# A two-layer decoder trunk with four mixers: every engine's queue ordered by a simulated timeline, and the first block rearranged

## The chip, the cores and the metric

The kernel runs on one core of one Trainium2 chip. The metric is the device time of one execution in microseconds (us), from the program's start to its end on the core. Several engines work side by side, each through its own queue in order: PE (TensorE, matmuls and transposes), DVE (VectorE), ACT (ScalarE), POOL (GpSimd) and SP (SyncE, which here only issues DMAs). PEld is PE's loading of weights.

## The reference

The reference is a decoder trunk of two layers over 512 positions with 1,024 features, all in float32. In each layer:

```python
u = rmsnorm(h, norm_w[l])
proj = einsum('bsd,de->bse', u, w_in[l])
ret_p, diff_p, ssd_p, ml_p = split_cols(proj, ...)
ret_out = retention_mixer(...) * silu(rz)
diff_out = diff_attention_mixer(...) * silu(dz)
ssd_out = _rms(ssd_mixer(...) * silu(sz)) * ssd_norm_w[l]
ml_out = mlstm_mixer(...) * silu(mz)
mix = concatenate([ret_out, diff_out, ssd_out, ml_out])
h = h + einsum('bse,ed->bsd', mix, w_out[l])
```

After the second layer comes one more RMSNorm. All four mixers are causal; the kernel computes them in four chunks of 128 positions.

## The kernel before

**Tiles.** The four token tiles h0 to h3 (128 positions x 1,024 features) stay on the chip. The input projection of a layer is cut into blocks of 512 columns, and each block into eight weight tiles of 128 x 512. Float32 is made up from two parts: ACT casts a weight tile to a shorter format (`whi`, L357, or L360 with a scale for the output projection), and DVE subtracts that from the original to get the rest (`wlo`, L358 and L361). The same is done to the normalised activations (`uh` L347, `ul` L348), and to the mixers' results (`mh`, `ml`, L623). A product of two tiles is three matmuls, whi with uh, whi with ul, and wlo with uh, all recorded at L127; transposes are at L131. Raw weights come in by DMA from SP, two tiles each (L366, tile `raw`).

**What sets the order.** PE's order is written by hand. `drive` runs generators against a planner's clock that `mm` and `tr` advance, and `later` and `spawn` put pieces of a mixer at a planned time between the projections' matmuls. In the body of the kernel only PE is scheduled by hand (`manual_schedule`); DVE, ACT, POOL and SP get their order from the tile scheduler, which ranks instructions by priority, raised in places with `high_priority`. That order is fixed when the program is built: on the chip each engine takes its queue from the front and waits on semaphores.

**The first block.** `start` makes the first projection block, "mv", with its own order on all engines, since nothing is there to hide its loads. Its weight tiles come as `z` (0 to 7). For each token tile t, `squares(t)` is ACT's sum of squares (L390), `scale(t)` the statistics on DVE (L395, L397) with a power on POOL (L240), `mul(t)` the scaling on DVE (L404, two halves `e`), `trans(t)` the transposes on PE (L131) with the split into uh and ul. `hi(k)` and `lo(k)` make the two parts of weight tile k (L414, L418) on the engine that is named, and `run(pr[t], n)` issues the next n-1 steps of token t's matmuls. The strings in `orders` say in which order a token uses the high (h) and low (l) parts. `warm(n)` in `setup` issues n matmuls of ones (L127), whose result isn't used. Tables for later come after the weights: `rows` and `w` (used at L313 and L304) and the convolution's `cv` (L295, L298).

**Places in the body that the prediction speaks of.** In differential attention, `diff_av` transposes the attention weights on PE and copies them out of a bank of PSUM, on DVE for even t (L1157). A later projection matmul needs that bank. Near it on DVE are L361, the end of `diff_fin` (L1184, L1186), and the gating by silu (ACT L542, DVE L544). In the SSD mixer, each chunk has eight L950 on DVE (one for each head), an exponential on ACT (L952), and a product with the scores on DVE (L954, two halves), on which the matmuls into `psacc` wait. POOL works for the same mixer with L941, L967 and L980, and for the rotary embedding with L605, beside DVE's L604 and L606 and ACT's L602; DVE adds up the chunk's result at L978, L992 and L995. In the mLSTM mixer the same part is played by L839, L841 on ACT and L846. The last token's final norm is at L1296 to L1304.

Of the kernel before, what the change touches and what calls it, by code (L numbers as in the profile page):

```python
# [99 lines left out]
class Trunk:  # L100
# [21 lines left out]
    def mm(self, out, lhsT, rhs, start=True, stop=True, share=1.0, **kw):  # L122
        n = 1
        for d in rhs.shape[1:]:
            n *= d
        self.clk += max(n, 64 if lhsT.dtype == F32 else 256) / 2400.0 * (4 if lhsT.dtype == F32 else 1) * share
        self.nc.tensor.matmul(out, lhsT=lhsT, rhs=rhs, start=start, stop=stop, **kw)  # L127
# [71 lines left out]
    def setup(self):  # L199
        nc = self.nc  # L200
        self.h = [self.hp.tile([P, D], F32, name=f"h{t}") for t in range(NT)]
        row = self.t("raw", [1, D], bufs=2)
        nc.scalar.dma_start(out=row, in_=self.nrm[0:1, :])
        for half in range(2):
            hs = slice(half * 512, (half + 1) * 512)
            nc.sync.dma_start(out=self.h[0][:, hs], in_=self.x[0:P, hs])
        cst = self.cp.tile([P, C_W], F32, name="cst")
        nc.sync.dma_start(out=cst[:, 0:P], in_=self.cst[:, 0:P])
        self.rest = lambda: nc.sync.dma_start(out=cst[:, P:], in_=self.cst[:, P:])
        self.c = lambda o, w, p=P: cst[:p, o:o + w]  # L210
        self.ident = self.c(C_ID, P)
        self.ones = self.cp.tile([P, P], F32, name="ones")
        nc.vector.memset(self.ones, 1.0)
        self.nhalf = self.cp.tile([P, 8], F32, name="nhalf")
        nc.vector.memset(self.nhalf, -0.5)
        self.zrow = self.cp.tile([4, P], F32, name="zrow")
        nc.vector.memset(self.zrow, 0.0)


        p = self.psum()  # L220

        def warm(n):
            for _ in range(n):
                self.mm(p[:, 0:P], lhsT=self.ones, rhs=self.ones)
        warm(4)
        self.nw = [self.psum() for _ in range(2)]
        for half in range(2):
            self.mm(self.nw[half], lhsT=self.ones[0:1, :], rhs=row[:, half * 512:(half + 1) * 512])
        warm(3)
        self.free(p)  # L230

    def setup2(self):
# [140 lines left out]
    def start(self, evac):  # L373

        nc = self.nc
        E = mybir.EngineType
        b = BIDX["mv"]
        w = [[None, None] for _ in range(KD)]
        us, ms, rs = {}, {}, {}

        def run(g, n=None):
            for i, _ in enumerate(g):
                if n and i == n - 1:
                    return

        def squares(t):
            ms[t] = self.sm([P, 2])
            for half in range(2):
                junk = self.t("e", [P, 512], BF16, bufs=4)
                nc.scalar.activation(junk, self.h[t][:, half * 512:(half + 1) * 512], AF.Square,  # L390
                                     accum_out=ms[t][:, half:half + 1])

        def scale(t):
            m = self.sm([P, 1])
            nc.vector.tensor_scalar(m, ms[t][:, 0:1], EPS * D, None, ALU.add)  # L395
            m2 = self.sm([P, 1])
            nc.vector.tensor_scalar(m2, ms[t][:, 1:2], m, 1.0 / D, ALU.add, ALU.mult)  # L397
            rs[t] = self.sm([P, 1])
            self.rsqrt(rs[t], m2, 1)

        def mul(t):
            us[t] = [self.ev(), self.ev()]
            for half in range(2):
                nc.vector.scalar_tensor_tensor(us[t][half], self.h[t][:, half * 512:(half + 1) * 512], rs[t],  # L404
                                               self.nw[half], ALU.mult, ALU.mult)

        def trans(t):
            for half in range(2):
                self.norm_tr(t, half, us[t][half])
            self.done.add(("u", 0, t))  # L410

        def hi(k, eng=nc.scalar.copy):
            w[k][0] = self.t("whi", [P, 512], F32R, bufs=10)
            eng(out=w[k][0], in_=raw[k])  # L414

        def lo(k, eng=nc.vector):
            w[k][1] = self.t("wlo", [P, 512], F32R, bufs=10)
            eng.tensor_tensor(out=w[k][1], in0=raw[k], in1=w[k][0].bitcast(F32), op=ALU.subtract)  # L418

        with self.tc.manual_schedule(engines={E.Activation, E.DVE, E.Pool, E.SP}):  # L420
            self.setup()
            load = lambda t: nc.sync.dma_start(out=self.h[t], in_=self.x[t * P:(t + 1) * P, :])
            raw = []
            for k in range(KD):
                raw.append(self.t("z", [P, 512], bufs=8))
                nc.sync.dma_start(out=raw[k], in_=self.win[0, b, :, k, :])
                if k == 1:
                    load(1)
            load(2)
            load(3)  # L430
            self.rest()
            self.loads(0)

            orders = ["h0 h1 l0 l1 h2 h3 h4 h6 l2 h5 l4 l3 h7 l6 l5 l7", "h0 h1 h2 h3 l0 l1 l2 l3 h4 h5 h6 h7 l4 l5 l6 l7"]
            pr = [self.proj_tok("mv", evac, w, (t,), [(int(x[1]), ("hl".index(x[0]),)) for x in orders[min(t, 1)].split()])
                  for t in range(NT)]
            squares(0)
            scale(0)
            mul(0)
            hi(0, nc.vector.tensor_copy)  # L440
            trans(0)
            lo(0)
            hi(1)
            hi(2)
            hi(3)
            lo(1)
            run(pr[0], 6)
            squares(1)
            hi(4, nc.vector.tensor_copy)
            hi(6, nc.vector.tensor_copy)  # L450
            lo(4, nc.gpsimd)
            scale(1)
            lo(2)
            hi(5)
            hi(7)
            mul(1)
            lo(6, nc.gpsimd)
            lo(3)
            run(pr[0], 6)
            trans(1)  # L460
            lo(5)
            lo(7, nc.gpsimd)
            run(pr[0], 2)
            squares(2)
            run(pr[1], 4)
            run(pr[0])
            scale(2)
            mul(2)
            run(pr[1], 4)
            squares(3)  # L470
            trans(2)
            scale(3)
            mul(3)
            self.free(*self.nw, lag=3.0)
            run(pr[1])
            self.gates_w()
            run(pr[2], 8)
            trans(3)
            run(pr[2])
            run(pr[3])  # L480
            self.setup2()
        yield
# [873 lines left out]
```

## Time and profile before

| | us |
|---|---|
| three runs | 1043.56, 1045.69, 1046.55 |
| median | 1045.69 |
| the profiled execution's own time | 1043.91 |
| its span, first to last instruction | 1042.1 |
| mean granted clock of TensorE | 0.994 |

The profile shows one execution. An interval in brackets behind a row of its timeline is the time that the engine stood idle ahead of it, with what ended the wait: "[2.13 <-DVE w L1157]" is 2.13 us, ended by DVE's tile w at L1157. "x3" merges three like instructions in a row, and the duration then spans all of them. Names of engines with a q (POOLq) are the engine's sequencer.

### The profile page before, as it was taken

The numbers are of one execution on the slowest core, as the hardware profiler recorded it, in microseconds if no ns is written. First come the engines' busy times: TensorE is split into PE (matmuls) and PEld (weight loads), VectorE is DVE, ScalarE is ACT, GpSimd is POOL, SyncE is SP. The second block draws the span as 40 slices with busy tenths as digits, with TensorE's granted clock in tenths as the row PEclk, the third lists the DMA queues.
The fourth block names the chain that finished last, engine by engine and source line by source line (L and its number), as shares of the span: only waits on it lengthen the run. The fifth ranks groups of instructions, "written<-read, shape, count | busy, mean of one in ns | idle before, by whom it ended". The sixth has DMA issues, their size and how long they took to land.

```text
span 1042.1 us, 14190 instructions
## 1 busy us (share of the span) xinstructions
PE 1023.0 (98%) x5110; PEld 835.1 (80%) x5110; DVE 693.2 (67%) x1495; ACT 479.7 (46%) x1057; POOL 164.9 (16%) x204
## 2 busy tenths in 40 slices
PE   8999999999999999999999999999999999999997
PEld 6788888877778887878887888887777888878786
DVE  5588675567787867446655967666667786863454
ACT  4444336545455444433343542575444553553332
POOL 2000132101111233022000012210001112510301
PEclk9999999999999999999999999999999999999999
DMA  7324322322212413313122422233121233233112
GB/s 254 107 72 122 102 71 82 101 82 81 79 44 85 128 51 102 102 61 126 41 84 80 138 85 81 82 101 103 60 86 56 81 100 103 81 102 101 42 60 81
DMA packets 39144, 93.84 MB, mean 90 GB/s; under 512 B 3849, under 2 KB 16777, under 8 KB 38946
## 3 DMA queue, kind: packets, MB, share of 16 engines
q1 hardware_dynamic: 38064, 91.49, 28.7%
q10 hardware_dynamic: 1010, 1.45, 0.4%
q8 instruction: 40, 0.66, 0.3%
q14 instruction: 30, 0.25, 0.1%
HBM read 90.78 MB, written 2.15 MB: 89 GB/s over the span
## 4 chain that ended last, share of the span: by engine, by line
PE 90%; DVE 5%; issue 1%; ACT 1%; DMA 1%; POOL 0%; POOLq 0%; DVEq 0%; ACTq 0%
PE pspj L127 74%; PE psS L127 6%; PE psacc L127 6%; PE psS L131 4%; DMA raw<-in_w_in_dram 1%; DVE wlo L361 1%; DVE w L950 1%; DVE ft L606 0%; DVE z L1291 0%; DVE wlo L358 0%; DVE h L657 0%; DVE z L544 0%; ACT e L253 0%; DMA raw<-in_w_out_dram 0%; DVE wlo L418 0%
## 5 line engine op out<-in xcount | busy, mean ns | idle before, releaser
L358 DVE TENSOR_TENSOR wlo<-raw,whi 128x512 fp32r<-128x512 f32 x248 | 174.0, 721 | 67.4 <-ACT whi L357 61.8
L127 PE MATMUL pspj<-whi,uh 128*128 128x512 f32 x512 | 209.7, 410 | 0.0
L127 PE MATMUL pspj<-whi,ul 128*128 128x512 f32 x512 | 200.9, 392 | 0.0
L127 PE MATMUL pspj<-wlo,uh 128*128 128x512 f32 x512 | 197.7, 393 | 2.4 <-DVE wlo L418 2.2
L357 ACT CAST whi<-raw 128x512 fp32r<-128x512 f32 x248 | 147.8, 618 | 108.5 <-PE pspj L127 60.8
L127 PE MATMUL pspj<-uh,whi 128*128 128x512 f32 x448 | 179.2, 400 | 0.0
L127 PE MATMUL pspj<-uh,wlo 128*128 128x512 f32 x448 | 174.7, 390 | 0.0
L127 PE MATMUL pspj<-ul,whi 128*128 128x512 f32 x448 | 174.6, 390 | 0.0
L127 PEld LDWEIGHTS pspj<-wlo,uh 128*128 128x128 f32 x512 | 96.5, 189 | 25.1 <-DVE wlo L418 3.9
L127 PEld LDWEIGHTS pspj<-whi,uh 128*128 128x128 f32 x512 | 97.0, 189 | 22.4 <-issue 3.0
L127 PEld LDWEIGHTS pspj<-whi,ul 128*128 128x128 f32 x512 | 96.9, 189 | 17.8 <-DVE ul L348 0.4
L127 PE MATMUL pspj<-whi,mh 128*128 128x512 f32 (+1 forms) x260 | 105.2, 405 | 4.3 <-DVE w L1157 4.3
L240 POOL TENSOR_TENSOR s<-s,nhalf 128x4 f32<-128x4 f32 (+1 forms) x44 | 35.8, 813 | 417.5 <-DVE s L1181 122.9
L127 PE MATMUL pspj<-whi,ml 128*128 128x512 f32 (+1 forms) x260 | 101.4, 390 | 0.3
L127 PE MATMUL pspj<-wlo,mh 128*128 128x512 f32 (+1 forms) x260 | 101.2, 389 | 0.0
L127 PEld LDWEIGHTS pspj<-uh,wlo 128*128 128x128 f32 x448 | 84.1, 188 | 18.2
L127 PEld LDWEIGHTS pspj<-uh,whi 128*128 128x128 f32 x448 | 84.2, 188 | 17.4 <-issue 0.7
L127 PEld LDWEIGHTS pspj<-ul,whi 128*128 128x128 f32 x448 | 84.3, 188 | 16.0
L584 DVE SCALAR_TENSOR_TENSOR e<-pspj,cvh,e 128x511 f32<-128x511 f32 (+2 forms) x90 | 67.0, 744 | 9.6 <-ACT e L582 8.4
L602 ACT ACTIVATE e<-pspj 32x512 f32<-32x512 f32 x96 | 56.6, 589 | 20.0 <-PE pspj L127 18.7
L657 DVE TENSOR_TENSOR h<-pspj,h 128x512 f32<-128x512 f32 (+1 forms) x65 | 43.6, 678 | 28.7 <-PE pspj L127 28.3
L127 PEld LDWEIGHTS pspj<-whi,mh 128*128 128x128 f32 x260 | 49.3, 190 | 15.4 <-DVE w L1157 5.2
(221 smaller groups left out, 1406.4 us busy)
## 6 DMA issues: line engine op xcount, KB each, us to landing
raw<-in_w_in_dram SPq DMA_DIRECT2D x116, 512.0 KB, 3.9
raw<-in_w_out_dram SPq DMA_DIRECT2D x32, 512.0 KB, 3.5
bcm<-adr SPq DMA_DIRECT2D x16, 256.0 KB, 3.3
z<-in_w_in_dram SPq DMA_DIRECT2D x8, 256.0 KB, 6.6
bcm<-gdr SPq DMA_DIRECT2D x8, 256.0 KB, 3.8
out_dram<-z SPq DMA_DIRECT2D x7, 256.0 KB, 2.0
h<-in_x_dram SPq DMA_DIRECT2D x3, 512.0 KB, 6.5
cst<-in_consts_dram SPq DMA_DIRECT2D x1, 1035.0 KB
```

Of the source, the lines that this page charges most:

```text
L127: self.nc.tensor.matmul(out, lhsT=lhsT, rhs=rhs, start=start, stop=stop, **kw)
L131: self.nc.tensor.transpose(out, src, self.ident if ident is None else ident)
L240: self.nc.gpsimd.tensor_tensor(out=out, in0=m, in1=self.nhalf[:, :n], op=ALU.pow)
L357: nc.scalar.copy(out=hi, in_=raw)
L358: nc.vector.tensor_tensor(out=lo, in0=raw, in1=hi.bitcast(F32), op=ALU.subtract)
L361: nc.vector.scalar_tensor_tensor(lo, raw, scale, hi.bitcast(F32), ALU.mult, ALU.subtract)
L584: nc.vector.scalar_tensor_tensor(acc[:, s:], p[:, 0:S - s], w[:, 3 - s:4 - s], acc[:, s:], ALU.mult, ALU.add)
L602: nc.scalar.activation(x[q * 32:q * 32 + 32, :], p[o * 32:o * 32 + 32, :], AF.Copy, scale=scale)
L657: nc.vector.tensor_tensor(out=hs, in0=p, in1=hs, op=ALU.add)
L950: nc.vector.scalar_tensor_tensor(e[:, j * P:(j + 1) * P], ab[g][:, j, :], self.ncs[:, t, h:h + 1], self.cap, ALU.add, ALU.min)
```

## The change

The diff has three parts. First, `schedule_with_timeline_sim=True`: the tile scheduler now picks, on each engine that isn't ordered by hand, the next instruction by a simulated timeline of all engines instead of by priority alone. Second, `warm(3)` in `setup` goes, so three of the seven matmuls of ones. Third, the first block's hand-written order changes: token 0 takes h7 ahead of its low parts 4, 6 and 3, the other tokens take all high parts before all low ones, the low parts 4 and 6 on POOL are issued behind `mul(1)` and `trans(1)`, and low part 7 goes from POOL to DVE.

```diff
--- before.py
+++ after.py
@@ -226,7 +226,6 @@
         self.nw = [self.psum() for _ in range(2)]
         for half in range(2):
             self.mm(self.nw[half], lhsT=self.ones[0:1, :], rhs=row[:, half * 512:(half + 1) * 512])
-        warm(3)
         self.free(p)
 
     def setup2(self):
@@ -431,7 +430,7 @@
             self.rest()
             self.loads(0)
 
-            orders = ["h0 h1 l0 l1 h2 h3 h4 h6 l2 h5 l4 l3 h7 l6 l5 l7", "h0 h1 h2 h3 l0 l1 l2 l3 h4 h5 h6 h7 l4 l5 l6 l7"]
+            orders = ["h0 h1 l0 l1 h2 h3 h4 h6 l2 h5 h7 l4 l6 l3 l5 l7", "h0 h1 h2 h3 h4 h5 h6 h7 l0 l1 l2 l3 l4 l5 l6 l7"]
             pr = [self.proj_tok("mv", evac, w, (t,), [(int(x[1]), ("hl".index(x[0]),)) for x in orders[min(t, 1)].split()])
                   for t in range(NT)]
             squares(0)
@@ -448,19 +447,20 @@
             squares(1)
             hi(4, nc.vector.tensor_copy)
             hi(6, nc.vector.tensor_copy)
-            lo(4, nc.gpsimd)
             scale(1)
             lo(2)
             hi(5)
             hi(7)
             mul(1)
+            run(pr[0], 5)
+            trans(1)
+            lo(4, nc.gpsimd)
             lo(6, nc.gpsimd)
             lo(3)
-            run(pr[0], 6)
-            trans(1)
+            run(pr[1], 4)
             lo(5)
-            lo(7, nc.gpsimd)
-            run(pr[0], 2)
+            lo(7)
+            run(pr[0], 3)
             squares(2)
             run(pr[1], 4)
             run(pr[0])
@@ -1349,7 +1349,7 @@
     for i, (shape, dtype) in enumerate(_OUTS):
         args.append(nc.dram_tensor(f"out_{i}_dram", shape, mybir.dt.from_np(np.dtype(dtype)),
                                    kind="ExternalOutput").ap())
-    with tile.TileContext(nc) as tc:
+    with tile.TileContext(nc, schedule_with_timeline_sim=True) as tc:
         trunk_kernel(tc, args)
     r = _run(nc, [arrays], core_ids=[0])
     return r.results[0]["out_0_dram"]
```

PE's instructions are the same but for those three matmuls, and behind the first block they stand in the same order. The line numbers of the changed kernel are one lower from L230 to the rearranged lines of `start` (L418 is L417 there) and the same behind those. The numbers of tiles in its rows are lower by 3 outside the first block.

The first place is PE in the first block, from the warm-up on; `e` are the normalised halves, `psS` the transposes' banks, `pspj_174` (171 in the changed kernel) is token 0's sum and `pspj_251` (236) token 1's. Before, from the low parts of token 0 to its end and the transposes of token 1:

```order
L127 MATMUL pspj_174<-wlo_202,uh_75 128x512
L127 MATMUL pspj_174<-whi_204,uh_75 128x512
L127 MATMUL pspj_174<-whi_204,ul_76 128x512
L127 MATMUL pspj_174<-wlo_194,uh_75 128x512
L127 MATMUL pspj_174<-wlo_214,uh_75 128x512
L131 MATMUL psS_225<-cst,e_208 128x128 x4
L131 MATMUL psS_232<-cst,e_209 128x128 x4
L127 MATMUL pspj_174<-whi_206,uh_75 128x512
L127 MATMUL pspj_174<-whi_206,ul_76 128x512
L127 MATMUL pspj_174<-wlo_212,uh_75 128x512
L127 MATMUL pspj_251<-whi_148,uh_75 128x512
L127 MATMUL pspj_251<-whi_148,ul_76 128x512
```

And after:

```order
L127 MATMUL pspj_171<-wlo_197,uh_75 128x512
L127 MATMUL pspj_171<-whi_199,uh_75 128x512
L127 MATMUL pspj_171<-whi_199,ul_76 128x512
L127 MATMUL pspj_171<-whi_201,uh_75 128x512
L127 MATMUL pspj_171<-whi_201,ul_76 128x512
L131 MATMUL psS_216<-cst,e_203 128x128 x4
L131 MATMUL psS_223<-cst,e_204 128x128 x4
L127 MATMUL pspj_236<-whi_145,uh_75 128x512
L127 MATMUL pspj_236<-whi_145,ul_76 128x512
L127 MATMUL pspj_236<-whi_163,uh_75 128x512
L127 MATMUL pspj_236<-whi_163,ul_76 128x512
L127 MATMUL pspj_236<-whi_165,uh_75 128x512
```

In between token 0's high parts and the transposes of token 1 stood wlo_202, wlo_194 and wlo_214, the low parts 2, 4 and 3; now only wlo_197, the low part 2, stands ahead of them.

On DVE the end of the first block's stage for token 2 (`s` are its statistics, `cvh` and `cv` the convolution's table, `e_271` and `e_276` its normalised halves) read before:

```order
L418 TENSOR_TENSOR wlo_239<-z_118,whi_204 128x512
L395 TENSOR_SCALAR s_60_265<-s_55_246 128x1
L314 TENSOR_SCALAR aneg_457<-aneg_457 128x8
L397 TENSOR_SCALAR s_61_267<-s_55_246,s_60_265 128x1
L304 TENSOR_TENSOR w_448<-w_129 128x128
L404 SCALAR_TENSOR_TENSOR e_271<-h_81,s_62_269,psS_100 128x512
L404 SCALAR_TENSOR_TENSOR e_272<-h_81,s_62_269,psS_101 128x512
L295 TENSOR_SCALAR cvh_445<-cv_131 128x80
L298 TENSOR_SCALAR cv_131<-cv_131 128x1
```

And after:

```order
L417 TENSOR_TENSOR wlo_234<-z_111,whi_167 128x512
L417 TENSOR_TENSOR wlo_245<-z_115,whi_199 128x512
L417 TENSOR_TENSOR wlo_247<-z_119,whi_201 128x512
L394 TENSOR_SCALAR s_60_270<-s_56_252 128x1
L313 TENSOR_SCALAR aneg_454<-aneg_454 128x8
L303 TENSOR_TENSOR w_445<-w_126 128x128
L294 TENSOR_SCALAR cvh_442<-cv_128 128x80
L297 TENSOR_SCALAR cv_128<-cv_128 128x1
L396 TENSOR_SCALAR s_61_272<-s_56_252,s_60_270 128x1
L403 SCALAR_TENSOR_TENSOR e_276<-h_81,s_62_274,psS_100 128x512
L403 SCALAR_TENSOR_TENSOR e_277<-h_81,s_62_274,psS_101 128x512
```

The two rows of the convolution's table (L295, now L294, and L298, now L297) moved ahead of the second row of statistics and of L404 (now L403), and two more low parts are made by DVE ahead of them.

In ACT's row of the same stage the two casts of the next block's first raw weights (L357) moved ahead of the copy of token 0's result (L567) and of token 3's squares (L390); token 2's casts to uh (L347) stand behind all of these, as before.

The next place is DVE in the first layer's differential attention, around the copy at L1157 that PE waits for (`w_2424`, in the changed kernel `w_2421`). Before:

```order
L361 SCALAR_TENSOR_TENSOR wlo_2485<-raw_2478,cv_131,whi_2484 128x512
L361 SCALAR_TENSOR_TENSOR wlo_2491<-raw_2488,cv_131,whi_2490 128x512
L361 SCALAR_TENSOR_TENSOR wlo_2495<-raw_2488,cv_131,whi_2494 128x512
L1184 TENSOR_TENSOR s_696_2378<-s_696_2378,s_694_2372 128x4
L544 SCALAR_TENSOR_TENSOR z_2431<-e_2429,pspj_2264 128x512
L1186 TENSOR_TENSOR w_2381<-psacc_2014,s_696_2378 128x512
L544 SCALAR_TENSOR_TENSOR z_2456<-e_2454,pspj_2385 128x512
L1157 COPY w_2424<-psS_2422 128x128
L1138 RECIPROCAL s_708_2415<-rsum_2275 128x1
L1139 SCALAR_TENSOR_TENSOR s_659_2276<-s_708_2415,rsum_2275,nlam_454 128x1
L1141 SCALAR_TENSOR_TENSOR w_2399<-w_2400,s_659_2276,w_2399 128x512
L358 TENSOR_TENSOR wlo_2778<-raw_2775,whi_2777 128x512
```

And after:

```order
L1133 TENSOR_REDUCE s_703_2395<-psS_2399 128x1
L544 SCALAR_TENSOR_TENSOR z_2428<-e_2426,pspj_2261 128x512
L1184 TENSOR_TENSOR s_696_2375<-s_696_2375,s_694_2369 128x4
L360 SCALAR_TENSOR_TENSOR wlo_2482<-raw_2475,cv_128,whi_2481 128x512
L360 SCALAR_TENSOR_TENSOR wlo_2488<-raw_2485,cv_128,whi_2487 128x512
L1186 TENSOR_TENSOR w_2378<-psacc_2011,s_696_2375 128x512
L1157 COPY w_2421<-psS_2419 128x128
L360 SCALAR_TENSOR_TENSOR wlo_2492<-raw_2485,cv_128,whi_2491 128x512
L1138 RECIPROCAL s_708_2412<-rsum_2272 128x1
L544 SCALAR_TENSOR_TENSOR z_2453<-e_2451,pspj_2382 128x512
L1139 SCALAR_TENSOR_TENSOR s_659_2273<-s_708_2412,rsum_2272,nlam_451 128x1
L1141 SCALAR_TENSOR_TENSOR w_2396<-w_2397,s_659_2273,w_2396 128x512
```

Ahead of the copy stood four L361 since L1181, and now three; the second L544 (z_2456, now z_2453) stood ahead of it, and is now two rows behind.

The last place is the SSD mixer's last chunk in the first layer. DVE before, from L978 to the second half of L954 and what follows:

```order
L978 TENSOR_TENSOR w_3812<-psacc_3809,g_144_575 128x512
L992 TENSOR_TENSOR state_3818<-psS_3815,state_3818 128x512
L950 SCALAR_TENSOR_TENSOR w_3838<-bcm_3822,g_148_583,cap 128x128 x2
L995 TENSOR_TENSOR w_3731<-psacc_3800,w_3731 128x512
L950 SCALAR_TENSOR_TENSOR w_3838<-bcm_3822,g_148_583,cap 128x128 x2
L950 SCALAR_TENSOR_TENSOR w_3845<-bcm_3824,g_148_583,cap 128x128 x4
L358 TENSOR_TENSOR wlo_4095<-raw_4092,whi_4094 128x512
L604 SCALAR_TENSOR_TENSOR ft_3865<-pspj_3763,cst 128x512
L954 TENSOR_TENSOR w_3838<-w_3838,psS_3835 128x512
L954 TENSOR_TENSOR w_3845<-w_3845,psS_3835 128x512
L606 TENSOR_TENSOR ft_3865<-ft_3865,e_3860 128x512
L358 TENSOR_TENSOR wlo_4099<-raw_4092,whi_4098 128x512
```

And after:

```order
L978 TENSOR_TENSOR w_3809<-psacc_3806,g_144_572 128x512
L992 TENSOR_TENSOR state_3815<-psS_3812,state_3815 128x512
L950 SCALAR_TENSOR_TENSOR w_3835<-bcm_3819,g_148_580,cap 128x128 x4
L950 SCALAR_TENSOR_TENSOR w_3842<-bcm_3821,g_148_580,cap 128x128 x4
L995 TENSOR_TENSOR w_3728<-psacc_3797,w_3728 128x512
L357 TENSOR_TENSOR wlo_4092<-raw_4089,whi_4091 128x512
L357 TENSOR_TENSOR wlo_4096<-raw_4089,whi_4095 128x512
L604 SCALAR_TENSOR_TENSOR ft_3862<-pspj_3760,cst 128x512
L954 TENSOR_TENSOR w_3835<-w_3835,psS_3832 128x512
L954 TENSOR_TENSOR w_3842<-w_3842,psS_3832 128x512
L313 TENSOR_SCALAR aneg_5003<-aneg_5003 128x8
```

The split wlo_4099 (now wlo_4096) moved from behind both L954 to ahead of L604, and L995 from among the L950 to behind them. POOL at the same place, before:

```order
L605 TENSOR_TENSOR e_3782<-e_3782,cst 128x512
L941 TENSOR_TENSOR w_3833<-w_3831,g_133_516 128x512
L980 TENSOR_TENSOR w_3731<-w_3731,w_3812 128x512
L967 TENSOR_TENSOR w_3852<-w_3831,rows_127 128x512
L605 TENSOR_TENSOR e_3860<-e_3860,cst 128x512
L240 TENSOR_TENSOR s_1290_3957<-s_1289_3955,nhalf 128x1
```

And after:

```order
L605 TENSOR_TENSOR e_3779<-e_3779,cst 128x512
L980 TENSOR_TENSOR w_3728<-w_3728,w_3809 128x512
L941 TENSOR_TENSOR w_3830<-w_3828,g_133_513 128x512
L967 TENSOR_TENSOR w_3849<-w_3828,rows_124 128x512
L605 TENSOR_TENSOR e_3857<-e_3857,cst 128x512
L239 TENSOR_TENSOR s_1290_3954<-s_1289_3952,nhalf 128x1
```

L941 and L980 changed places. In the second layer the same rows move in the same way.

## The prediction

> **What bounds the kernel now.** I read the page first (busy time by engine, then the chain that ended last), then the waits of PE, then the windows table for the granted clock, and then the timeline where PE stood still.
>
> ```profile
> PE 1023.0 (98%) x5110; PEld 835.1 (80%) x5110; DVE 693.2 (67%) x1495; ACT 479.7 (46%) x1057; POOL 164.9 (16%) x204
> ...
> PE 90%; DVE 5%; issue 1%; ACT 1%; DMA 1%; POOL 0%; POOLq 0%; DVEq 0%; ACTq 0%
> ...
> PE pspj L127 <- DVE w L1157: 4.3, 2, 2.2
> PE psacc L127 <- DVE w L954: 3.1, 2, 1.6
> PE pspj L127 <- DVE wlo L418: 2.2, 1, 2.2
> PE psS L127 <- DVE ones L213: 1.0, 1, 1.0
> PE psacc L127 <- DVE w L846: 0.7, 2, 0.3
> ```
>
> PE is busy for 98% of the span and makes 90% of the chain. Its waits (us in total, times, longest) add up to 4.3 + 3.1 + 2.2 + 1.0 + 0.7 = 11.3 us. The change takes nothing from PE but three small matmuls, so it can gain only in these waits, at the start, and in the clock. The clock is the second bound:
>
> ```profile
> 18.56:21.95 3.39, 3.39 (x12) 3.02 (x13) 0.95 (x2) 1.47 (x3) 0.00 (x0) 0.50 0.56 209
> ...
> 248.50:254.00 5.50, 3.37 (x17) 2.46 (x15) 5.43 (x12) 3.34 (x8) 1.71 (x4) 1.00 0.58 191
> ...
> 759.25:762.65 3.40, 3.32 (x8) 2.67 (x9) 2.74 (x6) 1.31 (x3) 1.06 (x3) 0.50 0.37 137
> ...
> 916.27:919.66 3.39, 3.39 (x10) 2.77 (x10) 1.84 (x6) 0.91 (x3) 0.56 (x1) 0.50 0.50 158
> ```
>
> The waits in the timeline (start, duration, then what was waited for):
>
> ```profile
> 251.25 0.50 PE L127 MATMUL pspj<-whi,mh 128*128 128x512 f32 x1 [2.13 <-DVE w L1157]
> ...
> 404.93 1.97 PE L127 MATMUL psacc<-w,w 128*128 128x64 f32 x16 [1.49 <-DVE w L954]
> ...
> 759.33 0.80 PE L127 MATMUL pspj<-whi,mh 128*128 128x512 f32 x1 [2.20 <-DVE w L1157]
> ...
> 914.63 2.16 PE L127 MATMUL psacc<-w,w 128*128 128x64 f32 x16 [1.60 <-DVE w L954]
> ```
>
> The column before the DMA share is the granted clock. Stretches of 3.4 us run at 0.50, right behind a stall of PE: the second layer's stalls at 759.33 and 914.63, not the first layer's twins at 251.25 and 404.93. Some 3.4 us at half speed cost half of that, up to 1.7 us; I use 1.5, since PE isn't at work for all of it. Whether a stall of 1.5 to 2.4 us is punished thus looks like a matter of how it lies to some fixed grid.
>
> By the Trainium skill, "TensorE: Matmul & The Clock Gate", section "HAM oscillation — how this bites in real kernels", only PE gaps above about 3.4 us re-throttle. The 2.20 us at 759.33 speaks against it. By that rule no stall of the changed kernel would be punished; this is the third rival.
>
> The profiled execution took 1043.91 us (span 1042.1); the three runs had 1043.56, 1045.69 and 1046.55. Their spread, 3.0 us, is two half-clock stretches of 1.5, so I take the median as the profiled execution plus about one (1.78 us above it). Sums below go against 1043.91.
>
> **The change part by part: the start.**
>
> ```profile
> 6.15 1.47 DVE L404 SCALAR_TENSOR_TENSOR e<-h,s,psS 128x512 f32<-128x512 f32 x2 [0.67 <-POOL s L240]
> ...
> 6.76 1.65 PE L127 MATMUL psS<-ones 128*128 128x128 f32 x6
> ...
> 8.20 1.92 PE L131 MATMUL psS<-cst,e 128*128 128x128 f32 x8
> ...
> 9.94 0.79 PE L127 MATMUL pspj<-whi,uh 128*128 128x512 f32 x1
> ...
> 11.82 0.39 PE L127 MATMUL pspj<-whi,ul 128*128 128x512 f32 x1
> ...
> 14.45 1.01 POOL L240 TENSOR_TENSOR s<-s,nhalf 128x1 f32<-128x1 f32 x1
> ...
> 15.49 1.40 DVE L404 SCALAR_TENSOR_TENSOR e<-h,s,psS 128x512 f32<-128x512 f32 x2 [0.45 <-POOL s L240]
> ...
> 16.82 1.66 DVE L418 TENSOR_TENSOR wlo<-z,whi 128x512 fp32r<-128x512 f32 x1
> ...
> 18.53 0.80 PE L127 MATMUL pspj<-wlo,uh 128*128 128x512 f32 x1 [2.24 <-DVE wlo L418]
> ...
> 19.12 1.91 PE L131 MATMUL psS<-cst,e 128*128 128x128 f32 x8
> ...
> 24.04 1.41 DVE L404 SCALAR_TENSOR_TENSOR e<-h,s,psS 128x512 f32<-128x512 f32 x2 [0.53 <-POOL s L240]
> ...
> 27.27 1.07 ACT L347 CAST uh<-psS 128x512 fp32r<-128x512 f32 x2
> ...
> cv<-in_conv_dram SPq DMA_DIRECT2D x1, 44.5 KB, 9.7
> ```
>
> The late warm-up ran from 6.76 to 8.41 (1.65 us), while the first e half was ready at 6.15 + 0.75 = 6.90. Without it the first transposes start at about 6.95 in place of 8.20, and the first projection matmul at 9.94 - 1.25 = 8.7. This lead doesn't last, because DMA feeds the weights one by one; what counts is where the stages for tokens 1 and 2 come to lie.
>
> Token 1: the rsqrt on POOL stood behind the low part of block 4 and took 1.01 us at 14.45. With that part moved behind it, it costs about 0.55 (DVE waits 0.53 for the same operation ahead of 24.04) and starts near 13.8; L404 follows about 0.8 us earlier, 14.7 to 16.1. Its transposes stood in PE's queue behind the low part 3, which DVE made at 16.82 in 1.66 us beside two such parts on POOL. In the new order no low part but 0 to 2 stands ahead of them, so they run at about 15.5 to 16.7 and not from 19.12 to 21.03: 3.6 us sooner, and the 2.24 us stall at 18.53 goes.
>
> Token 2 is late next. DVE's row of the new order puts L295 and L298, which need the convolution table, ahead of the statistics of token 2. That load takes 9.7 us from its issue at 11.75, so lands at 21.45; with 0.20 + 0.15 for the two, 0.21 for L397, 0.55 on POOL and some hand-overs L404 starts at about 22.8, in place of 24.04: 1.2 us. ACT now casts the first loaded weights and copies v before token 2's cast, so that cast moves from 27.27 to about 25.6, 1.7 us, and PE's first matmuls behind it gain with them, 1.7 to 2.2 us. I take **-2.0 us**, bounds -1 (only the lead of L404) to -3 (the stall of 2.24 and the rest of the 1.65). If the clock halves once more here the cost is 1.5; today it halves once (18.56), and I count that as kept.
>
> **Gap A, the copy at L1157, once in each layer.**
>
> ```profile
> 246.89 2.24 DVE L361 SCALAR_TENSOR_TENSOR wlo<-raw,cv,whi 128x512 fp32r<-128x512 f32 x3
> ...
> 250.31 0.68 DVE L544 SCALAR_TENSOR_TENSOR z<-e,pspj 128x512 f32<-128x512 f32 x1
> ...
> 250.91 0.29 DVE L1157 COPY w<-psS 128x128 f32<-128x128 f32 x1
> ```
>
> PE waits at 251.25 for this copy, 2.13 us. Before, DVE did all three L361 and the second L544 ahead of it; now one L361 (2.24 / 3 = 0.75) and that L544 (0.68) stand behind: 1.42 us less queue. ACT, whose results L1186 and L544 need, gives part of it back; I take 1.1 us per layer, bounds 0.5 to 1.4, so **-2.2 us**. The rest of the stall, about 1.1 us, should be too short to halve the clock: **-1.5** in the second layer, where it does today. The L361 moved behind the copy feeds a weight block that PE reads later; PE reads it some hundred rows later.
>
> **Gap B, L954 in the last token of the SSD mixer, once in each layer.**
>
> ```profile
> 395.54 1.04 POOL L941 TENSOR_TENSOR w<-w,g 128x512 f32<-128x512 f32 x1 [3.45 <-ACT w L938]
> ...
> 397.88 1.29 POOL L980 TENSOR_TENSOR w<-w,w 128x512 f32<-128x512 f32 x1 [1.29 <-DVE w L978]
> ...
> 398.25 2.12 DVE L950 SCALAR_TENSOR_TENSOR w<-bcm,g,cap 128x128 f32<-128x128 f32 x2
> ...
> 400.89 2.09 DVE L950 SCALAR_TENSOR_TENSOR w<-bcm,g,cap 128x128 f32<-128x128 f32 x6
> ...
> 404.11 1.27 DVE L954 TENSOR_TENSOR w<-w,psS 128x512 f32<-128x512 f32 x2
> ```
>
> Here the new order is worse. The split of weight half 4099 (0.68 us by the same spacing, L358) moves from behind L954 to ahead of it; L941 on POOL moves from 395.54, where it ran when DVE was in no L950, to behind L980. An L950 takes 1.06 us beside a POOL operation (2.12 / 2), and 2.09 / 6 = 0.35 without one, so one more POOL operation in that stretch holds up one more L950, by 0.7. Against it, DVE's L606 at 395.57 is freed of L941, and the eight L950 may begin up to 0.8 earlier. Sum 0.6 + 0.7 - 0.4 = 0.9 us per layer, **+1.8 us**; bounds 0.4 (all of the freed 0.8 counts) to 3.3 (POOL's four operations in one row, each also held by an L950). PE's stall grows from 1.49 to 2.4 us, as long as gap A's, so a halved clock behind it is likely in both layers: today in one, **+1.5**.
>
> By the Trainium skill, "SBUF — State Buffer", section "SBUF: two separate sides", DVE with two SBUF inputs and a GpSimd operation exclude each other for a whole instruction; the 1.06 against 0.35 agrees. Without such a lock L941's place would not matter, and gap B's term would be 0.2 per layer, the sum 1.4 us lower (0.7 per layer).
>
> **Places that should cost nothing.**
>
> ```profile
> 140.80 0.63 ACT L841 ACTIVATE w<-w 128x512 f32<-128x512 f32 x1 [2.12 <-DVE w L839]
> ...
> 141.47 0.69 DVE L846 SCALAR_TENSOR_TENSOR w<-psS,w 128x512 f32<-128x512 f32 x1 [0.70 <-ACT w L841]
> ...
> 1033.98 1.28 POOL L1296 TENSOR_TENSOR z<-h,bcm 128x512 f32<-128x512 f32 x1 [2.13 <-DVE h L657]
> ...
> 1034.82 0.72 DVE L1296 TENSOR_TENSOR z<-h,bcm 128x256 f32<-128x256 f32 x1
> ```
>
> At L846 (PE waits 0.35 us in each layer) a cast on ACT and a split on DVE now stand ahead. ACT is idle for 2.12 us before L841, and DVE for 0.70 before L846: the cast (0.6) and the split (0.68) fit there. If they come late, they cost up to 0.6 per layer; I take 0. In the last token, L1296 on DVE goes ahead of a statistic; today it ends at 1035.54, just after POOL's L1296 (1035.26), which holds it. It will end there again: 0.  GpSimd's low part 7 goes to DVE: 0.68 us there, in a stretch where PE has token 1's high parts to do; if that cover is gone, its 0.7 us are inside the start's bounds. SP's gathers (bcm, gdr) go out a place or two sooner, and no weight load stands behind a wait that PE shows today: 0.
>
> **The sum.** -2.0 - 2.2 - 1.5 + 1.8 + 1.5 = -2.4, so 1043.91 - 2.4 = 1041.5. Against the median of 1045.69 that is -4.2. I don't add the 1.78 by which the median lies above the profiled execution: I took it as one more halved stretch, and the sum already counts both gaps B as halved while gap A's are gone. Forecast: **1041.5 us**, its own range 1039.5 to 1043.5.
>
> **Rivals.** (1) *The clock takes the gain.* Both gaps B are punished, and the start or a rest of gap A once or twice more; a later grant of full speed (today between 9.94 and 11.82, where a matmul falls from 0.79 to 0.39) counts the same, since the warm-up that goes was work for PE just before it. Plus 1.5 to 3: about 1044. For it: three stretches at 0.50 in one execution; against: the long gap A goes. Chance 0.20. (2) *The reordering doesn't do what it says for PE*: gap A stays, because L1157 waits for ACT rather than for its queue, gap B keeps its length, and only the start gains: 1045.69 - 2.0 = 1043.7. For it: PE's row is the same behind the first block. Chance 0.12. (3) *No stall of the changed kernel is punished*: 1041.5 less the two stretches kept in gap B, 3.0: 1038.5. For it: the first layer's twin of gap A ran at 1.00 (248.50 to 254.00). Chance 0.11. (4) *Slower*: gap B grows to its upper bound because POOL's row and the L950 hold each other in turn: 3.3 us per layer gives -2.0 - 2.2 - 1.5 + 1.5 + 6.6 = 2.4, so 1046.3; and a stall of 4.8 us is longer than a 3.4 us stretch, so each layer pays a second one, 2 x 1.7: 1049.7. Without the second stretches it passes the median, 1.78 above the profiled time, from 3.0 us per layer on. For it: L950 already takes three times as long beside POOL; against: L606 is freed. Chance 0.09.
>
> **How the numbers follow.** The forecast has 0.48. What a measurement can tell from no change is about 0.3%, 3.1 us: below 1042.55 is faster, above 1048.83 slower. Of the forecast's chance 0.36 lies below 1042.55, with 0.11 of rival 3 and 0.03 of rival 1: faster 0.50. Slower is most of rival 4, 0.08. Same 0.42. The range 1037.5 to 1046.0 takes in rivals 1 to 3 and the bounds of the start and gap A; outside are rival 4 and part of rival 3.
>
> **What would show it.** Start: transposes of token 1 near 15.5 and no wait for a wlo of L417 (L418 before); token 2's cast near 25.6. Gap A: wait for L1157 near 1.1 us in place of 2.2. Gap B: wait for L954 near 2.4 us, with L950 near 1.06 us three or four times. Clock: stretches at 0.50 only behind L954 and at the start. I am wrong if gap A's wait stays, if L846 or a new line appears among PE's waits with over 1 us, or if PE waits for a weight load.

## The result, and the profile after

| | before | changed |
|---|---|---|
| median of 4 runs each (lowest to highest), us | 1044.62 (1039.93 to 1046.55) | 1053.79 (1052.82 to 1054.33) |
| ratio to before, 95% interval | | 1.0093, 1.0071 to 1.0115 |
| the profiled execution's own time, us | 1043.91 | 1054.14 |
| its span, us | 1042.1 | 1052.4 |

The kernel became slower by 9.2 us, 0.93%; the forecast was 1041.5 with a range of 1037.5 to 1046.0. The page of the changed kernel (busy time by engine, the chain that ended last) and PE's waits (us in all, times, longest):

```profile
PE 1029.6 (98%) x5104; PEld 837.7 (80%) x5104; DVE 697.9 (66%) x1496; ACT 479.8 (46%) x1057; POOL 171.4 (16%) x203
...
PE 84%; DVE 8%; DMA 4%; ACT 2%; issue 1%; SPq 0%; POOL 0%; POOLq 0%; DVEq 0%; ACTq 0%
...
PE psS L127 <- DVE ft L589: 6.3, 2, 3.3
PE psacc L127 <- DVE w L954: 3.5, 2, 1.8
PE pspj L127 <- DVE w L1157: 1.7, 2, 0.9
PE psS L127 <- DVE ones L213: 1.0, 1, 1.0
PE psS L127 <- ACT w L685: 0.9, 1, 0.9
PE psacc L127 <- DVE w L846: 0.8, 2, 0.4
```

PE is still busy for 98% of the span, yet its part of the chain fell from 90% to 84%: DVE and DMA took it. Two lines of 0.9 us and more are new, L589 (twice, up to 3.3 us) and L685. (The three matmuls of ones that went are six of PE's records, 5104 in place of 5110.) The waits sum to 15.7 us in the whole list, against 11.3 before: 4.4 of the 10.2 us between the two profiled executions. The clock has most of the rest. Windows table (stretch, busy time of PE, PEld, DVE, ACT and POOL, granted clock, DMA share, GB/s):

```profile
18.56:21.95 3.39, 3.39 (x17) 2.79 (x15) 2.40 (x9) 0.49 (x3) 0.00 (x0) 1.00 0.85 329
101.30:104.68 3.38, 3.38 (x10) 2.60 (x9) 0.78 (x2) 0.60 (x1) 0.00 (x0) 0.50 0.02 6
408.50:415.28 6.78, 6.78 (x24) 5.84 (x24) 3.07 (x7) 1.45 (x3) 1.83 (x2) 0.50 0.14 56
616.70:620.08 3.38, 3.38 (x10) 2.71 (x9) 1.10 (x2) 0.60 (x1) 0.00 (x0) 0.50 0.07 27
923.90:930.70 6.80, 6.80 (x25) 6.05 (x26) 3.21 (x7) 1.44 (x3) 1.26 (x2) 0.50 0.19 66
```

Before, three stretches of 3.4 us ran at 0.50, 10.2 us in all. Now it is 3.4 + 6.8 + 3.4 + 6.8 = 20.4 us, though the one at 18.56 is gone. Another 10.2 us at half speed cost up to half of that, 5.1. With the waits' 4.4 that makes 9.5 of the 10.2 us.

How much later the same matmul starts in the changed kernel than before, read from the two timelines:

| start before, us | start after, us | difference | what lies just ahead |
|---|---|---|---|
| 40.65 | 38.51 | -2.1 | the first block |
| 47.17 | 46.04 | -1.1 | the wait for L685 |
| 97.93 | 100.27 | +2.3 | the wait for L589, layer 1 |
| 251.25 | 254.23 | +3.0 | a half-clock stretch; gap A, shorter than before |
| 605.92 | 615.99 | +10.1 | gap B with two half-clock stretches; the wait for L589, layer 2 |
| 919.91 | 930.63 | +10.7 | the half-clock stretch at 616.70; gap A shorter and its stretch gone; gap B and its stretches longer |

The cause of the wait at 100.27 lies some 27 us earlier, on DVE. The timeline of the changed kernel (start, duration, engine, line; in brackets the engine's idle time ahead and what ended it):

```profile
71.75 0.38 SPq L813 DMA_DIRECT2D bcm<-gdr  x1
...
72.23 0.75 DVE L584 SCALAR_TENSOR_TENSOR e<-pspj,cvh,e 128x511 f32<-128x511 f32 x1
...
75.98 0.88 DVE L839 SCALAR_TENSOR_TENSOR w<-bcm,g,cap 128x128 f32<-128x128 f32 x3 [2.41 <-DMA bcm<-gdr]
76.78 0.74 DVE L584 SCALAR_TENSOR_TENSOR e<-pspj,cvh,e 128x510 f32<-128x510 f32 x1
77.44 0.34 DVE L839 SCALAR_TENSOR_TENSOR w<-bcm,g,cap 128x128 f32<-128x128 f32 x1
...
78.77 0.74 DVE L584 SCALAR_TENSOR_TENSOR e<-pspj,cvh,e 128x509 f32<-128x509 f32 x1
...
100.27 0.49 PE L127 MATMUL psS<-ft,ft 128*128 128x128 f32 x2 [3.28 <-DVE ft L589]
```

And the kernel before at the same instructions:

```profile
73.08 0.75 DVE L584 SCALAR_TENSOR_TENSOR e<-pspj,cvh,e 128x510 f32<-128x510 f32 x1
...
74.08 0.73 DVE L584 SCALAR_TENSOR_TENSOR e<-pspj,cvh,e 128x509 f32<-128x509 f32 x1
...
78.74 0.35 DVE L839 SCALAR_TENSOR_TENSOR w<-bcm,g,cap 128x128 f32<-128x128 f32 x1
...
97.25 1.16 PE L127 MATMUL psS<-ft,ft 128*128 128x128 f32 x8
```

L584 makes the taps of a convolution, three for each feature tile, eight tiles in a row, and each tile passes ACT (L582), DVE (three L584), ACT (L587) and DVE (L589). L839 belongs to the first mLSTM chunk, whose scores on PE come only when the last of those tiles is ready, so its result isn't needed for another 20 us. The new order puts three L839 ahead of the fourth tile's second L584. L839 needs a broadcast of the gates (`bcm`) that SP issued at 71.75; DVE stands for 2.41 us until it lands. That L584 starts at 76.78 in place of 73.08, while PE is 1.1 us earlier: 4.8 us late against PE. The chain through the other four tiles wins back some 1.3 us, and PE waits for the rest.

### The profile page after: what moved, and what is told of

Read it like the earlier page. It is cut to its first block, busy times and chain, and to the rows that moved or that the text cites. A ratio compares the mean times of both kernels' runs of the same rounds, so it can differ in the third digit from the quotient of the medians.

```text
span 1052.4 us, 14174 instructions
## 1 busy us (share of the span) xinstructions
PE 1029.6 (98%) x5104; PEld 837.7 (80%) x5104; DVE 697.9 (66%) x1496; ACT 479.8 (46%) x1057; POOL 171.4 (16%) x203
## 4 chain that ended last, share of the span: by engine, by line
PE 84%; DVE 8%; DMA 4%; ACT 2%; issue 1%; SPq 0%; POOL 0%; POOLq 0%; DVEq 0%; ACTq 0%
PE pspj L127 69%; PE psacc L127 6%; PE psS L127 5%; PE psS L131 3%; DMA raw<-in_w_in_dram 3%; DVE wlo L357 1%; DVE e L584 1%; DVE w L950 1%; DVE w L839 1%; DMA z<-in_w_in_dram 1%; ACT whi L356 0%; DVE h L657 0%; ACT e L252 0%; DVE z L1291 0%; DMA bcm<-gdr 0%
## 5 line engine op out<-in xcount | busy, mean ns | idle before, releaser
L357 DVE TENSOR_TENSOR wlo<-raw,whi 128x512 fp32r<-128x512 f32 x248 | 173.6, 715 | 71.5 <-ACT whi L356 62.8
L127 PE MATMUL pspj<-whi,uh 128*128 128x512 f32 x512 | 211.9, 414 | 0.4 <-ACT uh L346 0.3
L239 POOL TENSOR_TENSOR s<-s,nhalf 128x4 f32<-128x4 f32 (+1 forms) x44 | 39.2, 891 | 418.9 <-DVE s L1181 204.8
L584 DVE SCALAR_TENSOR_TENSOR e<-pspj,cvh,e 128x511 f32<-128x511 f32 (+2 forms) x90 | 66.9, 744 | 9.0 <-ACT e L582 8.3
L657 DVE TENSOR_TENSOR h<-pspj,h 128x512 f32<-128x512 f32 (+1 forms) x65 | 43.8, 677 | 25.1 <-PE pspj L127 24.8
```

The lines of the kernel that those rows point to most:

```text
L239: self.nc.gpsimd.tensor_tensor(out=out, in0=m, in1=self.nhalf[:, :n], op=ALU.pow)
L357: nc.vector.tensor_tensor(out=lo, in0=raw, in1=hi.bitcast(F32), op=ALU.subtract)
L584: nc.vector.scalar_tensor_tensor(acc[:, s:], p[:, 0:S - s], w[:, 3 - s:4 - s], acc[:, s:], ALU.mult, ALU.add)
L657: nc.vector.tensor_tensor(out=hs, in0=p, in1=hs, op=ALU.add)
```

## The experiments

Theory 1: DVE's queue is held at L839 by a load, in each layer, and with the half clock behind the stall this is the loss. Theory 2: the order as a whole brings the weights and their splits later. Theory 3: the rearranged start sets it off. In the first experiment a scheduling dependency, which adds no instruction, keeps L839 behind the tap that it followed before:

```diff
+    def behind(self, inst, other):
+        self.tc.add_manual_dep(inst.ins, other.ins.name, mybir.DependencyInfo(
+            mybir.DependencyClass.NoSync, mybir.DependencyReason.SCHED_ONLY))
...
-                nc.vector.scalar_tensor_tensor(w[:, h * P:(h + 1) * P], gb[:, h, :], self.al[:, t, h:h + 1], self.cap,
-                                               ALU.add, ALU.min)
+                d = nc.vector.scalar_tensor_tensor(w[:, h * P:(h + 1) * P], gb[:, h, :], self.al[:, t, h:h + 1], self.cap,
+                                                   ALU.add, ALU.min)
+                if t == 0:
+                    self.behind(d, self.taps[-3 * 4])
```

`self.taps` lists the L584 in the order of the code. The lines move by some numbers in such kernels; L590 is L589, L961 is L954 and L1164 is L1157 in this one. (The first L584 that is named is that of the fourth tile from the end, so the fifth of eight.)

> The changed kernel with one pin: the first mLSTM chunk's four L839 on DVE may not be placed ahead of the first L584 of the fifth convolution feature, which is where they stood before. Theory 1 (DVE's queue held by the bcm load at L839, the delay handed on through L584, ACT and L589 to PE's transposes of ft): both waits of PE for L589 (3.3 and 3.0 us) and the two half-clock stretches behind them (1.6 us each) go, so about 9.5 us less than the changed kernel's 1053.8, near 1044. Theory 2 (the convolution is late because the weight loads and their splits as a whole come later in the new order): PE still waits for L589 by over 2 us and the time stays above 1050.

It took 1045.03 us, ratio to before 1.0006 (0.9988 to 1.0024), and PE's waits in its profile begin with:

```profile
PE psacc L128 <- DVE w L961: 3.5, 2, 1.8
PE pspj L128 <- DVE w L1164: 1.7, 2, 0.9
PE psS L128 <- ACT w L686: 1.4, 1, 1.4
PE psacc L128 <- DVE w L853: 1.3, 4, 0.4
PE psS L128 <- DVE ft L590: 1.1, 2, 0.7
```

Nearly all of the loss went with the place of eight instructions: compared row by row, DVE's order in this kernel differs from the changed kernel's in the first chunk's four L839 of each layer and nowhere else. Theory 2 falls. The next two take the change apart: the second has the new start with the old rule of scheduling, the third the old start with the new rule.

```diff
-    with tile.TileContext(nc, schedule_with_timeline_sim=True) as tc:
+    with tile.TileContext(nc) as tc:
```

> The changed kernel without the timeline simulation: only the warm-up and the first block differ from before. Theory 1 (the loss lies in the order of the body): PE's lead of 2.1 us at the end of the first block shrinks to 1.1 at the gates' copy L685, which stands on ACT behind casts that wait for weight loads; nothing is lost later, no wait for L589, so about 1 us faster than before, -0.5 to -3 with the clock's stretches. Theory 3 (the rearranged start sets off the loss, since an earlier PE meets later loads): slower than before by several us.

It took 1042.23 us, ratio 0.9973 (0.9958 to 0.9989): 1.8 us faster than the 1044.03 of before in that session. The wait at L685 that was expected isn't among PE's waits; under the old rule that copy stands on ACT ahead of two of the casts.

```diff
-    with tile.TileContext(nc) as tc:
+    with tile.TileContext(nc, schedule_with_timeline_sim=True) as tc:
```

> The kernel before with the timeline simulation alone: old warm-up, old first block. Theory 1: the two waits for L589 are there, a little shorter or longer by the start's 1 us, with their half-clock stretches; about 1055, 9 to 12 us slower than before. Theory 3: like before, within 3 us.

It took 1053.47 us, ratio 1.0068 (1.0045 to 1.0092), with the same wait as the changed kernel:

```profile
PE psS L127 <- DVE ft L589: 6.4, 2, 3.3
```

So the loss comes with the new rule alone, and the start by itself is a gain. Theory 3 falls. The fourth asks what holds DVE there, the wait or the four operations' own time:

```diff
             w = self.pg()
+            if t == 0:
+                gb = self.c(C_DEC, 4 * P).rearrange("p (h s) -> p h s", h=4)
...
+                if t == 0:
+                    self.behind(d, self.taps[-3 * 5])
```

> The changed kernel, but the first mLSTM chunk's four L839 read a constant table that lies on the chip in place of the gates' broadcast, and are pinned behind the first L584 of the fourth feature, so ahead of its second as in the changed kernel. The gates' part of that chunk's decay is left out. DVE has the same work in the same place, but nothing to wait for there. Theory 1a (the load's wait of 2.4 us is what holds the queue): the wait for L589 falls from 3.3 to about 1 us, the half-clock stretch behind it goes, 1045 to 1047. Theory 1b (the four operations' own 1.4 us ahead of the convolution are what counts): the wait stays at 2 us or more, about 1051 or above.

It took 1044.87 us, ratio 1.0004 (0.9981 to 1.0027). All four (L846 in its numbering; L585 is L584) stand ahead of the second tap, and nothing waits:

```profile
72.08 0.75 DVE L585 SCALAR_TENSOR_TENSOR e<-pspj,cvh,e 128x511 f32<-128x511 f32 x1
72.75 1.13 DVE L846 SCALAR_TENSOR_TENSOR w<-cst,g,cap 128x128 f32<-128x128 f32 x4
...
74.40 0.74 DVE L585 SCALAR_TENSOR_TENSOR e<-pspj,cvh,e 128x510 f32<-128x510 f32 x1
...
97.60 0.49 PE L128 MATMUL psS<-ft,ft 128*128 128x128 f32 x2 [0.74 <-DVE ft L590]
```

PE's wait falls from 3.28 to 0.74. SP still issues the load (at 71.50), and the rest of DVE's order is the changed kernel's, so only the wait is gone. The load's wait holds the queue; the work that was moved ahead, 1.13 us, costs PE little: with it behind, in the first experiment, the wait was 0.67. The fifth puts the misplacement into the kernel before, without the new rule (the index is that of the second tap of the fourth tile, the fifth from the end):

```diff
+                if t == 0 and h == 2:
+                    self.behind(self.taps[-3 * 5 + 1], d)
```

> The kernel before (old warm-up, old first block, priority order) with one pin: the fifth convolution feature's second L584 may not be placed ahead of the first chunk's third L839. So the misplacement alone, without the timeline simulation. There L839 waits for the bcm load until about 78.7 us, so that L584 comes some 6 us later than at 73.08, and the chain wins back a little over 1 us until the transposes at 97. Theory 1 (this place alone makes the loss): a new wait of PE for L589 of 4 to 6 us in each layer and 1.6 to 3.4 us of half clock behind it, 1055 to 1062. Theory 2 (it takes the timeline order as a whole): below 1048.

It took 1056.35 us, ratio 1.0126 (1.0097 to 1.0154). DVE's timeline (L844 is L839) and PE's longest wait:

```profile
80.05 0.88 DVE L844 SCALAR_TENSOR_TENSOR w<-bcm,g,cap 128x128 f32<-128x128 f32 x3 [4.01 <-DMA bcm<-gdr]
80.84 0.74 DVE L585 SCALAR_TENSOR_TENSOR e<-pspj,cvh,e 128x510 f32<-128x510 f32 x1
```

```profile
PE psS L128 <- DVE ft L590: 7.9, 4, 3.2
```

The load is issued later in this order (75.60), so DVE stands for 4.01 us. The time was inside what theory 1 expected. The waits at L589, two in each layer (0.8 and 3.2 us in the first), come to 4.0 us a layer, the lower end of 4 to 6: that L584 starts 7.8 us late, and the chain won back more than the 1 us that was assumed. The half clock makes up the time: six stretches of 3.4 us in place of three. The scheduler answered the one pin with other moves as well, of splits and taps between 72 and 99 us and at the same place in the second layer, so this isn't the place alone as in the first experiment; but the old rule with this pin loses more than the changed kernel.

The last three go the other way. The sixth has the new start and the old rule, with pins that hold DVE's less urgent work behind the two instructions that PE waits for in gaps A and B:

```diff
+    def hold(self, inst, **n):
+        self.held = {k: [inst, *v] for k, v in n.items()}
+
+    def late(self, kind, inst):
+        first = self.held.get(kind)
+        if first and first[1]:
+            first[1] -= 1
+        elif first and first[2]:
+            first[2] -= 1
+            self.tc.add_manual_dep(inst.ins, first[0].ins.name, mybir.DependencyInfo(
+                mybir.DependencyClass.NoSync, mybir.DependencyReason.SCHED_ONLY))
...
-                nc.vector.tensor_copy(out=at[:, 0:n], in_=pa[:, 0:n])
+                d = nc.vector.tensor_copy(out=at[:, 0:n], in_=pa[:, 0:n])
+                if t == 0 and h == 1:
+                    self.hold(d, wlo_out=(4, 4), silu=(1, 1))
...
+                if t == NT - 1 and g == 1:
+                    self.hold(d, wlo=(8, 2), rope=(0, 1))
```

The pairs say how many of a kind pass freely and how many are then held: `wlo_out` are L360, `silu` L544, `wlo` L357, `rope` L604; in the second place `d` is L954.

> The second experiment's kernel (new start, priority order) with two kinds of pins on DVE: in the attention the four L360 splits behind L1157 and one L544 may not stand ahead of that copy, and in the last SSD chunk one L357 split and L604 may not stand ahead of L954. If the waits at L1157 (4.2 us in all) and L954 (3.1 us) are made by DVE's queue, as the prediction's gaps A and B had it, L1157's goes to about 0, L954's to about 0.7, and the half clock behind them becomes rare: 1042.2 - 4.2 - 2.4 - about 2 = 1033 to 1037. If ACT or POOL holds these instructions, less than 2 us are gained.

It took 1031.61 us (1030.77 to 1032.12), ratio 0.9889 (0.9867 to 0.9910): the fastest version, ahead of both kernels. PE's waits, and the copy (L1172 here, L361 the splits) in DVE's timeline:

```profile
PE psS L128 <- DVE ones L214: 1.0, 1, 1.0
PE pspj L128 <- ACT uh L347: 0.8, 2, 0.6
PE psacc L128 <- DVE w L967: 0.7, 2, 0.4
```

```profile
245.59 0.28 DVE L1172 COPY w<-psS 128x128 f32<-128x128 f32 x1
245.78 3.44 DVE L361 SCALAR_TENSOR_TENSOR wlo<-raw,cv,whi 128x512 fp32r<-128x512 f32 x4
```

L1157 is gone from the list and L954 (L967 here) fell to 0.7; no stretch at 0.50 is left but the one after the last matmuls. The time fell below the expected range: 10.6 us under the second experiment, where 6.6 were expected of the waits and 2 of the clock. The profiled executions of the two, both without a half-clock stretch ahead of the last matmuls, lie 7.5 us apart (1039.23 and 1031.76). That is the waits' part; the rest, 3 us, fits the clock, as the slower runs of the second experiment show a mean granted clock of 0.993 to 0.995 and its fastest three 0.998. The sixth's runs lie within 1.4 us of each other, those of before in that session within 7.6.

The seventh has the same holds and the first experiment's pin on the changed kernel.

> The changed kernel with the first experiment's pin on L839 and the same two kinds of pins at L1157 and L954. If the order by the timeline is good but for these three places, it comes to the time of the pinned priority order (1033 to 1037); the wait for L685 (1.4 us in the first experiment's profile) is left, so 1 to 2 us above it.

It took 1034.30 us, ratio 0.9915 (0.9893 to 0.9938). The wait for L685 (L687 here) is its longest:

```profile
PE psS L129 <- ACT w L687: 1.2, 1, 1.2
```

With the three places mended, the order by the timeline comes 2.7 us behind the pinned order by priority.

> The changed kernel with the three late warm-up matmuls put back. The prediction gave their removal a lead of 1.25 us for the first transposes that doesn't last, because DMA feeds the weights one by one: then the time is within 1 us of the changed kernel's 1053.8, and PE is as late at the end of the first block as without them. Rival: the lead lasts, and it is 1.3 to 1.7 us slower.

The eighth puts `warm(3)` back into the changed kernel:

```diff
+        warm(3)
         self.free(p)
```

It took 1052.11 us (1048.22 to 1055.55), ratio 1.0075 (1.0046 to 1.0105). That is 1.7 us under the changed kernel's 1053.79, taken in another session and with a spread of 7.3 us, so outside the 1 us that was expected, and on the side that no theory had. Nor is it the warm-up alone: with it back, the scheduler puts two splits (L358 here) on DVE ahead of token 2's L404; in the changed kernel they stand behind it (L403 there). From the profiled execution, the slowest of the six:

```profile
23.45 1.29 DVE L358 TENSOR_TENSOR wlo<-raw,whi 128x512 fp32r<-128x512 f32 x2 [1.43 <-ACT whi L357]
...
24.66 1.40 DVE L404 SCALAR_TENSOR_TENSOR e<-h,s,psS 128x512 f32<-128x512 f32 x2
...
25.55 1.29 PE L131 MATMUL psS<-cst,e 128*128 128x128 f32 x8 [1.88 <-DVE e L404]
```

In the changed kernel that L403 starts at 22.65 and these transposes at 23.54. Up to there the lead does shrink as expected: token 1's transposes start at 15.94 here and 15.72 there. What the three matmuls are worth in the end this run can't tell.

## Why the prediction was wrong

**The step that failed** is the one under "Places that should cost nothing": the forecast asked of the reordering only what it does to the waits that PE already had, and passed over the gathers with "SP's gathers (bcm, gdr) go out a place or two sooner ... 0". What was moved with them was their reader: L839 went ahead of the taps on DVE, whose queue then waits for the gather itself. A place in a queue was priced by the durations of the rows ahead (four L839, 1.2 us there), not by when those rows can start. The runs put the price of this place at some 9 us: 1053.79 against 1045.03 with the pin (before took 1044.62 and 1044.03 in the two sessions). In the profiled execution the two waits at L589 are 6.3 us, and the two half-clock stretches behind them, 6.8 us in all, cost up to 3.4. The point under what would make the forecast wrong, a new line among PE's waits with over 1 us, is what happened.

**The start** was right. Timeline of the changed kernel (L131 transposes, L403 and L346 what L404 and L347 were):

```profile
6.87 1.97 PE L131 MATMUL psS<-cst,e 128*128 128x128 f32 x8
...
15.72 1.26 PE L131 MATMUL psS<-cst,e 128*128 128x128 f32 x8
...
22.65 1.41 DVE L403 SCALAR_TENSOR_TENSOR e<-h,s,psS 128x512 f32<-128x512 f32 x2 [0.73 <-POOL s L239]
...
25.48 0.56 ACT L346 CAST uh<-psS 128x512 fp32r<-128x512 f32 x1
...
46.04 1.06 PE L127 MATMUL psS<-cst,w 32*128 32x16 f32 x8 [0.93 <-ACT w L685]
```

Forecast were 6.95, 15.5, 22.8 and 25.6, and a gain of 2.0; it is 2.1 at the end of the block. That the half-clock stretch at 18.56, which the forecast counted as kept, is gone too gave little of this: before, token 2's first half was ready at 24.8 and its transposes began at 25.24, so without the stretch PE could have been only some 0.4 us earlier (an estimate from these rows). One us is given back at 46.04: in the new order L685 stands on ACT behind casts that wait for weight loads. In the second and sixth experiments it stands ahead of two of these and PE doesn't wait there. The second experiment measured the start alone at -1.8 us.

**Gap A** was right: a wait of 0.86 us at 254.23, forecast 1.1, and no halved clock behind it. What the working missed is how much more was to be had, since the copy could run before the splits altogether.

```profile
254.23 0.50 PE L127 MATMUL pspj<-whi,mh 128*128 128x512 f32 x1 [0.86 <-DVE w L1157]
```

**Gap B** was mis-sized in both its terms, the wait and the clock.

```profile
399.23 5.53 DVE L950 SCALAR_TENSOR_TENSOR w<-bcm,g,cap 128x128 f32<-128x128 f32 x8
400.11 1.10 POOL L941 TENSOR_TENSOR w<-w,g 128x512 f32<-128x512 f32 x1
401.16 1.09 POOL L967 TENSOR_TENSOR w<-w,rows 128x512 f32<-128x512 f32 x1
402.21 1.34 POOL L605 TENSOR_TENSOR e<-e,cst 128x512 f32<-128x512 f32 x1
...
405.28 1.28 DVE L357 TENSOR_TENSOR wlo<-raw,whi 128x512 fp32r<-128x512 f32 x2
...
407.08 1.27 DVE L954 TENSOR_TENSOR w<-w,psS 128x512 f32<-128x512 f32 x2
407.90 1.42 PE L127 MATMUL psacc<-w,w 128*128 128x64 f32 x8 [1.65 <-DVE w L954]
```

The mechanism is there: eight L950 take 5.53 us beside four POOL operations in a row (L980 ahead of these three). But the wait grew only from 1.6 to 1.8 us at most, not to 2.4. In the first layer the L950 take 1.3 us more than before (5.53 against 2.12 and 2.09) and the split adds 0.6. Against that the first L950 starts 1.8 us sooner against the moment when PE stands ready (403.44 before, 406.25 now): 0.9 of it is the freed L606 (0.68 in place of 1.56 us), and 1.0, which the working didn't have, comes from DVE's row as a whole, which begins that much sooner against PE. The forecast took 0.4 for this side. The clock's term, +1.5 in all, was too small in this execution: behind each of the two waits lie 6.8 us at 0.50, 13.6 in all, which cost half of that, 6.8; before, it was 3.4 us behind one of them, 1.7. So +5.1 in place of +1.5. In the first experiment's profile the same waits drew none. So a halved stretch isn't a cost that belongs to a stall, and the forecast of a single execution can be off by several us through it.

The traces show what decides, and that the prediction's guess of a fixed grid was right. In all ten profiles the granted clock changes only at whole multiples of 3.413 us behind the moment when it first rose: in the changed kernel at 101.28, 408.48, 616.69 and 923.89, which is 26, 116, 177 and 267 times 3.413 behind 12.53. Cut the ten profiles into these windows and take those at full clock. Where PE's rows fill less than 1.5 us of a window, the next one was halved in 12 cases of 12; at 1.5 to 2.0 us in 10 of 16; above that in 1 of 2,939. The changed kernel's wait for L954 (406.25 to 407.90) lies whole in one window, 405.06 to 408.48, and the next is halved. The first experiment's wait at the same place (403.92 to 405.66) is split by a border at 405.33, and none is. The first rise, and with it every border, lay anywhere from 9.78 to 12.80 us in the ten profiles.

**The clock as such** was read rightly as a second bound. The rule of the Trainium skill, "TensorE: Matmul & The Clock Gate", section "HAM oscillation — how this bites in real kernels", that only gaps above some 3.4 us throttle, doesn't hold in these runs: 1.65 us at 407.90 is followed by 6.8 us at 0.50. The third rival, built on it, is refuted by the changed kernel, and the first one had the right mechanism for part of the loss but not its cause.

## What to carry to other kernels

A reordering of an engine's queue is to be checked instruction by instruction for the moment when each can start: one that needs a load, placed ahead of a chain that feeds the busiest engine, costs the load's wait and not its own duration. The waits that the profile shows say where an order can gain, not where a new one can lose; for that, look for readers of DMA that moved ahead of work with a deadline. A few scheduling dependencies at the two places of each layer where the busiest engine waits were worth 10.6 us here, on top of the new start's 1.8; the new rule for the whole order lost 9 without them.

## What the hardware showed unexpectedly

The granted clock stayed at half for 6.8 us, not 3.4, behind both stalls at L954 of the changed kernel (408.50 and 923.90), where PE's work right after the stall is sixteen matmuls of 64 columns; behind the stalls at L589, which are longer (3.28 us), it was 3.4 us. Four stalls in the ten profiles were followed by 6.8 us, all four at L954, and there the first halved window begins 0.1 to 0.6 us behind the first of the sixteen. Behind three other stalls at L954, in the kernel before and the fifth experiment, it begins 1.4 to 1.6 us behind it, with most of them done, and the clock was at half for 3.4 us. Whether those small matmuls count too little as work was not tried. Stalls of the same length drew a half clock in some executions and none in others, by their place in the grid. The first experiment's twelve runs spread over 8.5 us (1040.58 to 1049.12), the sixth's six over 1.4.
